# A routed-expert stage: 4 KB weight runs, low parts on VectorE, earlier gathers, and two accumulators taken by turns

## The chip, the cores and the metric

The kernel runs on one core of a Trainium2 chip. A core has TensorE (PE in the profile; PEld is its loading of the stationary operand), VectorE (DVE), ScalarE (ACT), GpSimd (POOL) and SyncE (SP), each with an instruction queue of its own that it works through in order, and 16 DMA engines that all queues share. The metric is the device time of one execution in microseconds (us); times given are medians of several runs.

## The reference

One encoder block of width 1024 over 1024 tokens: a mixer (a long convolution and a state-space branch, gated), a layer norm, a mixture of 64 experts with a shared expert, and a second layer norm. The change touches the mixture and the last norm. Every token picks 8 of 64 experts; an expert has three matrices, gate and up of 1024x256 and down of 256x1024.

```
def step(acc, blk):
    tok, wt, e = blk
    xb = h_pad[tok]
    hb = jax.nn.silu(xb @ w_gate[e]) * (xb @ w_up[e])
    yb = (hb @ w_down[e]) * wt[:, None]
    return acc.at[tok].add(yb.astype(acc.dtype)), None

ffn = routed + shared
h = layer_norm(DN_ALPHA * h + ffn, ln2_g[i], ln2_b[i])
```

All of it is float32, 3 MB of weights for each expert, 201 MB in all.

## The kernel before

The kernel runs the mixer, then a merge stage (`merge`, with the shared expert and the router inside it), then the expert stage (`moe`), then the last norm. Float32 products are made from rounded operands: each operand is split into a high part (a rounded copy, made by ScalarE) and a low part (the operand less its high part), and a product of two operands is three matmuls, high by high, high by low and low by high (`mm3`, L76; called from L78 to L80 in the profile).

The expert stage runs 96 blocks of token rows. The experts are sorted by load and get fixed capacities of 192, 160, 128 and 112 rows. An expert of 192 or 160 rows makes two blocks, of 128 and of 64 or 32 rows; the others make one. `order` takes a heavy and a light expert by turns, so three blocks (128 rows, 64 or 32 rows, 128 or 112 rows) and two experts form a group that repeats 32 times. A small block packs high and low tokens into one stationary operand and needs two matmuls in place of three (`both_mm`, L1857; L1860 to L1863).

The weights of expert i come as three pieces of 1 MB, numbered p = 3i, 3i+1, 3i+2: half of gate and up, the other half, and down. `w_load(p)` (L1584) reads the expert's number into a register, issues the DMAs and fills one of six `eraw` buffers. For gate and up it writes 256 gate columns and 256 up columns of a row next to each other, so each contiguous run is 1 KB. Gate and up are issued by SP, down by POOL. `w_hi(p)` (L1602) makes the high part on ScalarE, and `w_lo(p)` (L1613) the low part, on VectorE for gate and up and on POOL for down.

`gather(b)` (L1620) fetches a block's rows from `h` in HBM by an indirect DMA from POOL into one of three `xg` buffers. `xpose(b)` (L1629) turns them on TensorE (L1640) and splits them. `swi_gu` and `both_gu` do gate and up (8 steps k), `swi_act` and `both_act` the activation, `hidden(b)` (L1645) turns and splits the result `hb`, and `down(b)` (L1650 to L1663) makes the output rows `yo` (two buffers) and adds them to `acc` in HBM by an indirect DMA from POOL that reads, adds and writes. A scatter waits until the one before it has landed, since both touch `acc`. `slot_tables` (L2056) makes the row numbers of eight experts at a time, a step in each block, on VectorE and TensorE.

Every engine's order is the order of the code in this stage (`manual_schedule`). In iteration b of the loop at L1718 it is: gather(b+3); high parts of pieces 2b+2 and 2b+3; gate and up of block b, and after k = 3 the low part of 2b+2, the load of 2b+8 and hidden(b-1); the activation of b; xpose(b+2); the low part of 2b+3 and the load of 2b+9; one table step; down(b-1) with its scatter.

The last norm (L1750 on) loads the 8 row tiles of `acc` (4.2 MB) as `fx` and, tile by tile, takes statistics, centres, scales and stores. Ahead of the stage, `early` (L1674) loads the first three pieces, makes the first tables and gathers block 0 while the merge stage still runs.

Of the kernel before, what the change touches and what calls it, by code (L numbers as in the profile page):

```python
# [41 lines left out]
class Kern:  # L42
# [1167 lines left out]
    def merge(self):  # L1210
# [5 lines left out]
        self.acc_d = self.scratch("acc", (L + P, D))  # L1216
        p1 = tc.alloc_tile_pool(name="mg", bufs=1, reuse_waits="tile")
# [99 lines left out]
        with ExitStack() as cx:  # L1317
# [138 lines left out]
            def sh_gu(t):  # L1456
                gu = [sh[k // 2][k % 2] for k in range(8)]
                for k, ps in enumerate(self.swi_gu(lhs(t), gu, P)):
                    if k < 7:
                        yield  # L1460
                yield self.swi_act(pool, ps, P, ld()[:, 0:256])
# [100 lines left out]
    def moe(self):  # L1562
# [3 lines left out]
        with ExitStack() as cx:  # L1566
# [17 lines left out]
            def w_load(p):  # L1584
                if p >= 192:
                    return
                i, q = divmod(p, 3)
                eng = nc.gpsimd if q == 2 else nc.sync
                if q != 1:
                    weng[0] = eng.value_load(self.eid[0:1, order[i]:order[i] + 1], min_val=0, max_val=63)  # L1590
                g, u, d = [a[n][0][bass.ds(weng[0], 1)].rearrange("o (p j) c -> (o p) j c", p=P)
                           for n in ("exp_w_gate", "exp_w_up", "exp_w_down")]
                parts = ((g[:, 0:4], u[:, 0:4]), (g[:, 4:8], u[:, 4:8]), (d,))[q]
                wraw[p] = rps[i % 2].tile([P, 2048], F32, name="eraw", bufs=3)
                v = wraw[p].rearrange("p (k c) -> p k c", k=parts[0].shape[1])
                c0 = 0
                for src in parts:
                    n = src.shape[2]
                    eng.dma_start(v[:, :, c0:c0 + n], src)
                    c0 += n  # L1600

            def w_hi(p, c=slice(0, 2048)):  # L1602
                if p >= 192:
                    return
                if p not in whl:
                    i, q = divmod(p, 3)
                    hi, lo = whl[p] = [wps[i % 2].tile([P, 2048], F32R, name=f"e{c}", bufs=3) for c in ("hi", "lo")]
                    k = 2 if q == 2 else 4
                    wsplit.setdefault(i, []).extend(zip(*[[v.rearrange("p (k c) -> p k c", k=k)[:, j] for j in range(k)]
                                                          for v in (hi, lo)]))  # L1610
                nc.scalar.copy(whl[p][0][:, c], wraw[p][:, c])  # L1611

            def w_lo(p, c=slice(0, 2048)):  # L1613
                if p >= 192:
                    return
                eng = nc.gpsimd if p % 3 == 2 else nc.vector
                hi, lo = whl[p]
                eng.tensor_tensor(lo[:, c], wraw[p][:, c], hi[:, c].bitcast(F32), ALU.subtract)  # L1618
# [31 lines left out]
            def down(b):  # L1650
# [3 lines left out]
                y = pool.tile([P, D], F32, name="yo", bufs=2)  # L1654
                wd = [[(h[:, q * 512:(q + 1) * 512], l[:, q * 512:(q + 1) * 512]) for q in range(2)] for h, l in wsplit[i][8:10]]
                if n in (32, 64):
                    self.both_down(hbs.pop(b), wd, y, n)
                else:
# [3 lines left out]
                    out=self.acc_d, out_offset=bass.IndirectOffsetOnAxis(ap=tabs[r][s][1], axis=0),  # L1662
# [11 lines left out]
            def early(oh):  # L1674
                er = tc.alloc_tile_pool(name="er0", bufs=1, side="right")
                rps.append(er)
                for p in range(3):
                    w_load(p)
                for _ in self.slot_tables(er, groups[0], tabs, 2, oh):
                    yield 2  # L1680
                gather(0)
                for _ in self.slot_tables(er, groups[1], tabs, 2, oh):
                    yield 3
# [20 lines left out]
            for p in range(3, 6):  # L1704
                w_load(p)
            xpose(0)
            for p in range(2):
                for c in [slice(c * 512, c * 512 + 512) for c in range(4)]:
                    w_hi(p, c)
                    w_lo(p, c)  # L1710
                w_load(p + 6)
            xpose(1)
            tj = iter(())

            def lo_load(p):
                w_lo(p)
                w_load(p + 6)
            for b, (i, r, s, o, n) in enumerate(blocks):  # L1718
# [5 lines left out]
                gather(b + 3)  # L1724
# [3 lines left out]
                for k, ps in enumerate((self.both_gu if n in (32, 64) else self.swi_gu)(x, gu, n)):  # L1728
                    if k == 3:
                        lo_load(2 * b + 2)  # L1730
                        hidden(b - 1)
# [4 lines left out]
                xpose(b + 2)  # L1736
                lo_load(2 * b + 3)
# [17 lines left out]
            for i in range(8):  # L1755
                nc.sync.dma_start(xs[i], self.acc_d[i * P:(i + 1) * P, :])
# [5 lines left out]
            def stats(i, h):  # L1762
                if h == 0:
                    st[i] = pool.tile([P, 2, 6], F32, name="f_st", bufs=2)
                nc.vector.bn_stats(st[i][:, h, :], xs[i][:, h * 512:(h + 1) * 512])  # L1765
# [57 lines left out]
    def swi_gu(self, lhs, gu, n):  # L1823
        ps = self.bank()
        for k in range(8):
            self.mm3(ps[:n, :], lhs[k][0], lhs[k][1], gu[k][0], gu[k][1], k == 0, k == 7)
            yield ps
# [37 lines left out]
    def both_gu(self, x, gu, n):  # L1865
        ps = self.bank()
        for k in range(8):
            self.both_mm(ps, x[:, k], n, gu[k][0], gu[k][1], k == 0, k == 7)
# [502 lines left out]
```

## Time and profile before

| | us |
|---|---|
| median of 3 runs | 3530.07 (3528.78 to 3532.55) |
| the profiled execution | 3534.84 |
| its span, first to last instruction | 3533.2 |
| PE, DVE, ACT, POOL busy over the span | 3188.0, 2590.6, 1406.7, 1676.7 |
| experts, from the first expert matmul to the last scatter's issue | 2395 to 3479 |
| last norm | 3479 to 3533 |

The profile comes from one execution, with a trace of every instruction and DMA packet. Busy shares say how much of a stretch an engine worked; what sets the time of a stretch is read from the idle time ahead of an instruction and from what released it. The clock column is the share of TensorE's full speed that was granted: 1.0 is 2.4 GHz, 0.5 is 1.2 GHz.

### The profile page before, as it was taken

The numbers are of one execution on the slowest core, as the hardware profiler recorded it, in microseconds if no ns is written. First come the engines' busy times: TensorE is split into PE (matmuls) and PEld (weight loads), VectorE is DVE, ScalarE is ACT, GpSimd is POOL, SyncE is SP. The second block draws the span as 40 slices with busy tenths as digits, with TensorE's granted clock in tenths as the row PEclk, the third lists the DMA queues.
The fourth block names the chain that finished last, engine by engine and source line by source line (L and its number), as shares of the span: only waits on it lengthen the run. The fifth ranks groups of instructions, "written<-read, shape, count | busy, mean of one in ns | idle before, by whom it ended". The sixth has DMA issues, their size and how long they took to land. (4 is left out here: it accounts for less than half of the span.)

```text
span 3533.2 us, 42386 instructions
## 1 busy us (share of the span) xinstructions
PE 3188.0 (90%) x14923; PEld 2506.6 (71%) x14923; DVE 2590.6 (73%) x3551; ACT 1406.7 (40%) x2206; POOL 1676.7 (47%) x1480
## 2 busy tenths in 40 slices
PE   8989998989998998899999999997889888888893
PEld 6767776777777777567888888875666666666662
DVE  6787887888787878557994344657778787677786
ACT  3334333343334232322223212415656555565663
POOL 2545454555454546441110320215667667777774
PEclk9999899999999999899999999988999999899996
DMA  4323232322322322744325445327999899888894
GB/s 131 78 72 87 67 96 75 85 73 79 91 78 75 89 72 91 215 147 151 106 90 173 126 155 158 107 85 242 271 271 270 259 259 262 250 249 249 250 283 128
DMA packets 439908, 538.22 MB, mean 152 GB/s; under 512 B 24361, under 2 KB 373325, under 8 KB 430989
## 3 DMA queue, kind: packets, MB, share of 16 engines
q1 hardware_dynamic: 404717, 379.23, 36.6%
q0 software_dynamic: 33824, 152.06, 15.0%
q10 hardware_dynamic: 1152, 4.19, 0.3%
q8 instruction: 119, 1.95, 0.2%
q14 instruction: 96, 0.79, 0.1%
HBM read 430.29 MB, written 105.12 MB: 152 GB/s over the span
## 5 line engine op out<-in xcount | busy, mean ns | idle before, releaser
L170 PE MATMUL bankA<-xth,whi 128*128 128x512 f32 (+1 forms) x1424 | 470.1, 412 | 0.5 <-ACT whi L73 0.3
L170 PE MATMUL bankA<-xtl,whi 128*128 128x512 f32 (+1 forms) x1424 | 452.6, 400 | 0.0
L170 PE MATMUL bankA<-xth,wlo 128*128 128x512 f32 (+1 forms) x1424 | 449.4, 397 | 1.5 <-POOL wlo L74 1.5
L1618 DVE TENSOR_TENSOR elo<-eraw,ehi 128x2048 fp32r<-128x2048 f32 (+1 forms) x134 | 393.7, 2945 | 18.9 <-ACT ehi L1611 13.1
L1661 POOL DMA_INDIRECT scr_acc<-yo,sidx x96 | 231.1, 2407 | 275.9 <-DMA scr_acc<-yo,sidx 147.1
L1611 ACT CAST ehi<-eraw 128x2048 fp32r<-128x2048 f32 (+1 forms) x198 | 356.3, 1852 | 3.3 <-DMA eraw<-in_exp_w_gate_dram 3.3
L74 POOL TENSOR_TENSOR wlo<-wraw,whi 128x1024 fp32r<-128x1024 f32 (+1 forms) x89 | 225.4, 2532 | 278.1 <-ACT whi L73 278.1
L170 PEld LDWEIGHTS bankA<-xtl,whi 128*128 128x128 f32 (+1 forms) x1424 | 274.5, 193 | 64.1 <-DVE xtl L74 0.4
L170 PEld LDWEIGHTS bankA<-xth,wlo 128*128 128x128 f32 (+1 forms) x1424 | 272.2, 191 | 64.5 <-POOL wlo L74 2.0
L170 PEld LDWEIGHTS bankA<-xth,whi 128*128 128x128 f32 (+1 forms) x1424 | 268.2, 195 | 58.3 <-issue 5.4
L1618 POOL TENSOR_TENSOR elo<-eraw,ehi 128x2048 fp32r<-128x2048 f32 x64 | 298.1, 4658 | 15.8 <-ACT ehi L1611 14.7
L399 POOL TENSOR_SCALAR Wm<-cbm,dt 128x128 f32<-128x128 f32 x256 | 129.9, 507 | 348.2 <-DVE cbm L373 348.2
L1625 POOL DMA_INDIRECT xg<-scr_h,gidx x96 | 182.3, 1899 | 63.4 <-issue 24.3
L79 PE MATMUL bankA<-elo,xgh 128*128 128x512 f32 (+1 forms) x512 | 203.6, 398 | 8.6 <-DVE elo L1618 8.6
L78 PE MATMUL bankA<-ehi,xgh 128*128 128x512 f32 (+1 forms) x512 | 210.1, 410 | 0.0
L80 PE MATMUL bankA<-ehi,xgl 128*128 128x512 f32 (+1 forms) x512 | 203.3, 397 | 0.0
L1640 PE MATMUL bankB<-ident,xg 128*128 128x128 f32 (+3 forms) x768 | 113.4, 295 | 94.0 <-DMA xg<-scr_h,gidx 92.5
L1640 PEld LDWEIGHTS bankB<-ident,xg 128*128 128x128 f32 (+3 forms) x768 | 101.5, 198 | 122.9 <-issue 107.5
L74 DVE TENSOR_TENSOR xgl<-bankB,xgh 128x512 fp32r<-128x512 f32 (+1 forms) x128 | 81.3, 664 | 107.7 <-ACT xgh L73 106.0
L80 PE MATMUL bankA<-ehi,hb 128*128 128x512 f32 (+1 forms) x256 | 121.3, 474 | 27.0 <-DVE hb L74 26.9
L1877 DVE SCALAR_TENSOR_TENSOR lows<-lows,wt 64x256 f32<-64x256 f32 (+1 forms) x32 | 132.5, 4140 | 15.5 <-ACT lows L1876 15.5
L393 DVE SCALAR_TENSOR_TENSOR Em<-bcs,Acs,Em 128x128 f32<-128x128 f32 x256 | 140.9, 609 | 2.3
(551 smaller groups left out, 7672.7 us busy)
## 6 DMA issues: line engine op xcount, KB each, us to landing
eraw<-in_exp_w_gate_dram SPq DMA_DIRECT2D x128, 512.0 KB, 5.9
eraw<-in_exp_w_down_dram POOLq DMA_DIRECT2D x64, 1024.0 KB, 6.0
eraw<-in_exp_w_up_dram SPq DMA_DIRECT2D x128, 512.0 KB
wraw<-in_w_in_dram SPq DMA_DIRECT2D x88, 512.0 KB, 4.1
bcs<-scr_at SPq DMA_DIRECT2D x128, 256.0 KB, 5.6
scr_K<-kout SPq DMA_DIRECT2D x32, 512.0 KB, 2.8
Kt<-scr_K SPq DMA_DIRECT2D x32, 512.0 KB, 3.5
scr_gate<-accf SPq DMA_DIRECT2D x16, 512.0 KB, 4.2
```

The costliest lines, as they stand in the source:

```text
L74: (lo_eng or nc.vector).tensor_tensor(lo, src, hi.bitcast(F32), ALU.subtract)
L78: mm(out, sh, mh, start=first, stop=False)
L79: mm(out, sh, ml, start=False, stop=False)
L80: mm(out, sl, mh, start=False, stop=last)
L170: mm(ps[h], wt[:, k, :n], x[:, h * 512:(h + 1) * 512], start=(k == 0 and f == 1), stop=(k == KT - 1 and l == 1))
L393: STT(E[:, h], bcs[:, 1, h], self.A[:, c, 32 + j:33 + j], E[:, h], ALU.subtract, ALU.min)
L1611: nc.scalar.copy(whl[p][0][:, c], wraw[p][:, c])
L1618: eng.tensor_tensor(lo[:, c], wraw[p][:, c], hi[:, c].bitcast(F32), ALU.subtract)
L1625: nc.gpsimd.indirect_dma_start(out=t[:n, :], out_offset=None, in_=self.h_d, in_offset=bass.IndirectOffsetOnAxis(ap=tabs[r][s][0], axis=0))
L1640: nc.tensor.transpose(ps[:, j * P:j * P + n], free(t[:n, k:k + 1], [[8, P]]), self.ident[:n, :n])
L1661: nc.gpsimd.indirect_dma_start(out=self.acc_d, out_offset=bass.IndirectOffsetOnAxis(ap=tabs[r][s][1], axis=0), in_=y[:n, :], in_offset=Non ...
L1877: nc.vector.scalar_tensor_tensor(t[:, 0:256], t[:, 0:256], w, t[:, 256:512], ALU.mult, ALU.mult)
```

## The change

1. Gate and up land in the buffer as one run each: a partition's 4 rows of 256 columns stay together, 4 KB to a run, gate ahead of up. The matmuls read the moving operand as two runs of 256 columns (`"p (s k c) -> p k s c"`); the shared expert's views get the same shape.
2. All three pieces are issued by SP, and all low parts are made by VectorE.
3. `eraw` has five buffers instead of six (the load of p+5 follows the low part of p); `yo` has four instead of two.
4. gather(b+5) stands behind xpose(b+2), in place of gather(b+3) at the iteration's start; two more gathers precede the loop.
5. hidden(b-1) stands ahead of the low part of 2b+2. In the two blocks of every eighth expert a second table step runs after k = 5.
6. Blocks scatter by turns into `acc` (odd b) and a new `ace` (even b), which is filled with zeros ahead of the stage: one memset and 8 stores of 512 KB. The zeros lie in the `xg` buffer that gather(0) uses.
7. The last norm loads 8 tiles of `ace` and then 8 of `acc`, and adds them on VectorE in 16 instructions of 128x512.

```
-                eng = nc.gpsimd if q == 2 else nc.sync
-                if q != 1:
+                eng = nc.sync
+                if q == 0:
...
-                wraw[p] = rps[i % 2].tile([P, 2048], F32, name="eraw", bufs=3)
-                v = wraw[p].rearrange("p (k c) -> p k c", k=parts[0].shape[1])
-                c0 = 0
-                for src in parts:
-                    n = src.shape[2]
-                    eng.dma_start(v[:, :, c0:c0 + n], src)
-                    c0 += n
+                wraw[p] = rps[p % 5 // 3].tile([P, 2048], F32, name="eraw", bufs=3 - p % 5 // 3)
+                v = wraw[p].rearrange("p (s k c) -> p s k c", s=len(parts), k=parts[0].shape[1])
+                for n, src in enumerate(parts):
+                    eng.dma_start(v[:, n], src)
...
-                eng = nc.gpsimd if p % 3 == 2 else nc.vector
                 hi, lo = whl[p]
-                eng.tensor_tensor(lo[:, c], wraw[p][:, c], hi[:, c].bitcast(F32), ALU.subtract)
+                nc.vector.tensor_tensor(lo[:, c], wraw[p][:, c], hi[:, c].bitcast(F32), ALU.subtract)
...
-                y = pool.tile([P, D], F32, name="yo", bufs=2)
+                y = pool.tile([P, D], F32, name="yo", bufs=4)
...
-                    out=self.acc_d, out_offset=bass.IndirectOffsetOnAxis(ap=tabs[r][s][1], axis=0),
+                    out=self.acc_d if b % 2 else self.ace_d,
+                    out_offset=bass.IndirectOffsetOnAxis(ap=tabs[r][s][1], axis=0),
...
+                z = er.tile([P, D], F32, name="xg")
+                nc.gpsimd.memset(z, 0.0)
+                for t in range(8):
+                    nc.sync.dma_start(self.ace_d[t * P:(t + 1) * P, :], z)
...
             def lo_load(p):
                 w_lo(p)
-                w_load(p + 6)
+                w_load(p + 5)
...
-                gather(b + 3)
...
                     if k == 3:
+                        hidden(b - 1)
                         lo_load(2 * b + 2)
-                        hidden(b - 1)
+                    if k == 5 and i % 8 == 0:
+                        next(tj, None)
...
                 xpose(b + 2)
+                gather(b + 5)
                 lo_load(2 * b + 3)
...
-            for i in range(8):
-                nc.sync.dma_start(xs[i], self.acc_d[i * P:(i + 1) * P, :])
+            xe = [pool.tile([P, D], F32, name="fe", bufs=8) for _ in range(8)]
+            for v, d in ((xe, self.ace_d), (xs, self.acc_d)):
+                for i in range(8):
+                    nc.sync.dma_start(v[i], d[i * P:(i + 1) * P, :])
...
-                nc.vector.bn_stats(st[i][:, h, :], xs[i][:, h * 512:(h + 1) * 512])
+                c = slice(h * 512, (h + 1) * 512)
+                TT(xs[i][:, c], xs[i][:, c], xe[i][:, c], ALU.add)
+                nc.vector.bn_stats(st[i][:, h, :], xs[i][:, c])
```

## Rows read from the trace of the kernel before

**Rows 1.** Windows: us, busy us of each engine (x instructions), PEclk, DMA share, GB/s.

```profile
2430.00:3430.00 1000.00, 879.35 (x4430) 661.91 (x4429) 772.68 (x762) 597.29 (x746) 701.50 (x298) 0.93 0.89 259
2600.00:2700.00 100.00, 88.56 (x428) 67.85 (x426) 78.72 (x76) 59.91 (x73) 72.00 (x31) 0.93 0.94 274
```

**Rows 2.** Window of the merge stage, ahead of the experts.

```profile
1500.00:2200.00 700.00, 696.83 (x3066) 556.55 (x3065) 428.21 (x575) 169.40 (x329) 131.35 (x115) 1.00 0.43 139
```

**Rows 3.** Groups by line, 2430 to 3430: busy us, mean ns, idle before.

```profile
L1618 DVE TENSOR_TENSOR elo<-eraw,ehi 128x2048 fp32r<-128x2048 f32 x120 | 363.5, 3032 | 13.2 <-ACT ehi L1611 13.1
L1611 ACT CAST ehi<-eraw 128x2048 fp32r<-128x2048 f32 x180 | 333.5, 1904 | 0.0
L1618 POOL TENSOR_TENSOR elo<-eraw,ehi 128x2048 fp32r<-128x2048 f32 x59 | 272.5, 4619 | 1.1
L1661 POOL DMA_INDIRECT scr_acc<-yo,sidx x90 | 218.4, 2427 | 255.6 <-DMA scr_acc<-yo,sidx 147.1 <-DVE sg L1834 25.9 <-ACT yo L1660 22.5
L1625 POOL DMA_INDIRECT xg<-scr_h,gidx x90 | 176.1, 1956 | 27.6 <-issue 23.4 <-PE bankB L1640 3.7 <-PE bankA L80 0.3
L1877 DVE SCALAR_TENSOR_TENSOR lows<-lows,wt 64x256 f32<-64x256 f32 (+1 forms) x29 | 124.4, 4291 | 14.1 <-ACT lows L1876 14.1
```

**Rows 4.** Waits, 2430 to 3430: us in total, times, longest.

```profile
POOL scr_acc L1661 <- DMA scr_acc<-yo,sidx: 147.1, 32, 8.0
DVE xgl L74 <- ACT xgh L73: 104.0, 33, 6.2
PE bankB L1640 <- DMA xg<-scr_h,gidx: 91.2, 35, 5.5
PE bankA L80 <- DVE hb L74: 18.6, 17, 1.9
```

**Rows 5.** Timeline: start us, us, engine, line, operation, [idle before <-releaser].

```profile
2427.22 0.48 DVE L1877 SCALAR_TENSOR_TENSOR lows<-lows,wt 64x256 f32<-64x256 f32 x1 [0.48 <-ACT lows L1876]
2902.72 4.59 POOL L1661 DMA_INDIRECT scr_acc<-yo,sidx  x1 [0.84 <-DMA scr_acc<-yo,sidx]
2903.54 2.27 DVE L1618 TENSOR_TENSOR elo<-eraw,ehi 128x2048 fp32r<-128x2048 f32 x1
2916.50 1.46 POOL L1661 DMA_INDIRECT scr_acc<-yo,sidx  x1 [6.41 <-DMA scr_acc<-yo,sidx]
```

**Rows 6.** Timeline of PE in two stretches with hardly a wait.

```profile
2430.64 0.43 PE L78 MATMUL bankA<-ehi,xgh 128*128 128x512 f32 x1
2436.92 1.09 PE L1640 MATMUL bankB<-ident,xg 64*128 64x64 f32 x8
2440.08 0.40 PE L78 MATMUL bankA<-ehi,xgh 128*128 128x512 f32 x1
...
3418.83 1.12 PE L1640 MATMUL bankB<-ident,xg 112*128 112x112 f32 x8 [0.22 <-DMA xg<-scr_h,gidx]
3422.57 0.39 PE L1861 MATMUL bankA<-ehi,xgh 128*64 128x512 f32 x1
3426.70 1.13 PE L1640 MATMUL bankB<-ident,xg 128*128 128x128 f32 x8
```

**Rows 7.** DMA queues, 2450 to 3350: packets, MB, share of 16 engines.

```profile
q0 software_dynamic: 26059, 121.11, 46.0%
q1 hardware_dynamic: 112143, 111.37, 43.2%
```

**Rows 8.** DMA queues, 3490 to 3497: the final loads, 4 KB rows.

```profile
q1 hardware_dynamic: 781, 2.88, 101.5%
```

**Rows 9.** Timeline and window of the tail.

```profile
3485.47 3.76 SPq L1756 DMA_DIRECT2D fx<-scr_acc  x8
3490.00:3494.00 4.00, 0.00 (x0) 0.00 (x0) 3.81 (x13) 0.44 (x2) 0.00 (x0) 0.50 1.00 402
```

**Rows 10.** Window and timeline of PE ahead of the stage.

```profile
2372.00:2376.00 4.00, 4.00 (x42) 3.31 (x41) 2.97 (x3) 0.00 (x0) 0.00 (x0) 1.00 0.01 2
2369.26 0.38 PE L1640 MATMUL bankB<-ident,xg 128*128 128x128 f32 x2
```

More of the change, by code (lines that the diff above doesn't have):

```diff
@@ L1216, in merge @@
         self.acc_d = self.scratch("acc", (L + P, D))
+        self.ace_d = self.scratch("ace", (L + P, D))
         p1 = tc.alloc_tile_pool(name="mg", bufs=1, reuse_waits="tile")
@@ L1456, in sh_gu @@
             def sh_gu(t):
-                gu = [sh[k // 2][k % 2] for k in range(8)]
+                gu = [[v.rearrange("p (s c) -> p s c", s=2) for v in sh[k // 2][k % 2]] for k in range(8)]
                 for k, ps in enumerate(self.swi_gu(lhs(t), gu, P)):
@@ L1607, in w_hi @@
                     hi, lo = whl[p] = [wps[i % 2].tile([P, 2048], F32R, name=f"e{c}", bufs=3) for c in ("hi", "lo")]
-                    k = 2 if q == 2 else 4
-                    wsplit.setdefault(i, []).extend(zip(*[[v.rearrange("p (k c) -> p k c", k=k)[:, j] for j in range(k)]
+                    k, n = (2, 1) if q == 2 else (4, 2)
+                    wsplit.setdefault(i, []).extend(zip(*[[v.rearrange("p (s k c) -> p k s c", s=n, k=k)[:, j] for j in range(k)]
                                                           for v in (hi, lo)]))
@@ L1653, in down @@
                 i, r, s, o, n = blocks[b]
-                y = pool.tile([P, D], F32, name="yo", bufs=2)
-                wd = [[(h[:, q * 512:(q + 1) * 512], l[:, q * 512:(q + 1) * 512]) for q in range(2)] for h, l in wsplit[i][8:10]]
+                y = pool.tile([P, D], F32, name="yo", bufs=4)
+                wd = [[(h[:, 0, q * 512:(q + 1) * 512], l[:, 0, q * 512:(q + 1) * 512]) for q in range(2)] for h, l in wsplit[i][8:10]]
                 if n in (32, 64):
@@ L1703, in moe @@
             gather(2)
-            for p in range(3, 6):
+            for p in range(3, 5):
                 w_load(p)
             xpose(0)
+            gather(3)
             for p in range(2):
@@ L1710, in moe @@
                     w_lo(p, c)
-                w_load(p + 6)
+                w_load(p + 5)
             xpose(1)
+            gather(4)
             tj = iter(())
@@ L1716, in lo_load @@
                 w_lo(p)
-                w_load(p + 6)
+                w_load(p + 5)
             for b, (i, r, s, o, n) in enumerate(blocks):
@@ L1824, in swi_gu @@
         ps = self.bank()
+        p3 = ps[:n, :].rearrange("p (s c) -> p s c", s=2)
         for k in range(8):
-            self.mm3(ps[:n, :], lhs[k][0], lhs[k][1], gu[k][0], gu[k][1], k == 0, k == 7)
+            self.mm3(p3, lhs[k][0], lhs[k][1], gu[k][0], gu[k][1], k == 0, k == 7)
             yield ps
@@ L1866, in both_gu @@
         ps = self.bank()
+        p3 = ps.rearrange("p (s c) -> p s c", s=2)
         for k in range(8):
-            self.both_mm(ps, x[:, k], n, gu[k][0], gu[k][1], k == 0, k == 7)
+            self.both_mm(p3, x[:, k], n, gu[k][0], gu[k][1], k == 0, k == 7)
             yield ps
```

## The prediction

> **What bounds the kernel now.** I read the windows first, to see which stage the change touches and whether any engine is full there. From 2430 to 3430 us the stage is in its steady state: 90 of its 96 blocks, by the 90 gathers [rows 3], so 30 groups of three blocks in 1000 us, 33.3 us each. PE is busy 879 us, DVE 773, POOL 702, ACT 597, the DMA engines 0.89, the granted clock 0.93 [rows 1]. Nothing is full, so the time lies in waits.
>
> The second view is a dense piece of PE's timeline, which gives the floor. A big block's gate and up take 6.28 us from their first matmul to the transposes behind them, and from there to the next block's first matmul (transposes, a table step, a small down) 3.16 us, 9.44 us together. A small block's gate and up take 4.13 us, and transposes with a big down 3.74 us [rows 6]. A group has one iteration of each kind: 9.44, 6.28 + 3.74 = 10.02, and 4.13 + 3.74 = 7.87, so 27.3 us without a wait.
>
> The third view is the list of waits: it must account for 33.3 - 27.3 = 6.0 us. PE waits for gathered rows 91.2 us in 30 groups, 3.0 each, and for `hb` 18.6 us, 0.6 each [rows 4]. The clock is the rest: 0.93 in place of 1.00 is 7% of 33.3, 2.3 us. The sum is 5.9. In the merge stage, where PE is busy 697 of 700 us, the clock is 1.00 [rows 2]; it falls in the expert stage, where PE waits.
>
> Why do rows come late? POOL's queue. It waits 147.1 us for an earlier scatter to land, at most 8.0 at once [rows 4]; 6.41 us before the one at 2916.50 [rows 5]. A gather stands behind it in POOL's queue, and so do POOL's low parts, 4.62 us each [rows 3]. A second effect is on VectorE: a low part takes 2.27 us where POOL makes none [rows 5] but 3.03 on average, and the product in `both_act` 0.48 us [rows 5] against 4.29 on average [rows 3]. Both read two SBUF operands and are held while POOL makes its own.
>
> **The change, part by part.**
>
> *Two accumulators, early gathers, four `yo` buffers.* A scatter now waits for the one two blocks back, about 20 us earlier, so the 147 us go. gather(b+5) leaves three iterations ahead of its use instead of nearly two. It gains a wait, on xpose(b+2), which frees its buffer; the scatter of b-1 queues behind that, and its data come later anyway. With some 28 us of lead I take the 3.0 us wait for rows as gone. Late next are `hb`, the clock and the DMA engines.
>
> *Low parts of down on VectorE.* It adds 59 x 2.27 = 134 us in the window. It removes the holding: 120 x (3.03 - 2.27) = 91 us, and 29 x (4.29 - 0.48) = 110 us [rows 3, 5]. VectorE's work falls from 772.7 / 30 = 25.8 to 23.5 us a group, and POOL's from 23.4 to 14.3. PE's cover for a low part is one iteration, as before. Placing hidden(b-1) ahead of a low part takes 2.27 us from the path to `hb`, but ScalarE's two high parts (1.90 us each [rows 3]) still stand ahead of it, so I keep the whole 0.6 us. The spaced table steps add no work; if one pushes the next `hb` back, its 0.6 us doubles, and the DMA term below still ends later.
>
> *4 KB runs, down on SP, five `eraw` buffers.* From 2450 to 3350 us (27 groups) queue q1, gate and up, holds the DMA engines for 43.2% and q0 for 46.0% [rows 7]: 14.4 and 15.3 us a group, 29.7 together. Per MB q1 costs 0.432 x 900 x 16 / 111.37 = 55.9 engine-us. The final loads, in 4 KB rows with nothing beside them, cost 1.015 x 7 x 16 / 2.88 = 39.5 [rows 8]. The price among scatters is in no row: between 39.5 (q1 falls to 10.2) and 55.9 (no gain). A gain beyond the first is excluded, since that stretch had no rival traffic; a loss I exclude too, as each run only has fewer ends. I take the middle, as the second figure contains queueing, which stays: q1 12.3 and 27.6 a group, ends 25.5 and 29.7. The Trainium skill, "DMA: Bandwidth & Descriptors", section Specifications, gives 512 B as the smallest transfer at line rate, by which 1 KB and 4 KB runs cost the same and the sum would be rival A's; the rows here mix run length with company and don't decide it. The highest share of the DMA engines over 100 us is 0.94 [rows 1]; at that the group needs 29.4 us, ends 27.1 and 31.6. Down moves to SP's queue at the same bytes. SP waits for VectorE's low part before each load, and what queues behind it are later loads alone. The shortest lead is now 1.3 iterations, about 13 us; ScalarE's high parts wait 0.0 us for weights today [rows 3], so I price the sixth buffer at nothing. The matmuls' view has one break in 512 columns. The nearest row, transposes with a stride at every element, 8 in 1.09 us [rows 6], runs on without gaps, so nothing there either.
>
> *Sum for a group.* PE: 27.3 + 0.6 for `hb` + a third of the clock's 2.3, since most of its falls follow the waits for rows, 0.8: 28.7. DMA: 29.4. The later counts: 29.4, so 3.9 us saved, times 32 groups, 125 us.
>
> *Ahead of the stage.* Eight zero stores (4.2 MB) go out behind the first weights, where the DMA engines are idle, share 0.01 [rows 10]: nothing. But gather(0) now waits for them, and PE turns its rows at 2369 us, in front of merge matmuls [rows 10]. If that order stays, PE could stand until about 2388, 19 us; if the compiler's order moves too, nothing. I take nothing; 19 is the upper end. A gain is excluded.
>
> *The tail.* The norm's first tile needs the ninth load instead of the first. Loads start at 3485.47 and run at up to 402 GB/s [rows 9], so 4.19 MB cost 10.4 us. If the `ace` loads pass ahead of the last scatter, nothing. Sixteen additions: a quarter of a low part, 0.57 us [rows 5], is the lower end; with some overhead 0.65, so 10.4 us. VectorE leads there, busy 3.81 of 4 us [rows 9], and nothing hides them. Tail: +21, ends +9 and +28 (two holds by POOL's additions, 3.6 us each, on top).
>
> **Sum.** 3534.8 - 125 + 21 = 3431 for a profiled run. The profiled run lies 4.8 us over the median of 3530.07, so 3426. Low: a group at 28.0 saves 170, tail +9, so 3369. High: a group at 31.6 saves 54, tail +21, so 3497; a late start as well is rarer than the range needs.
>
> **The rivals.**
>
> *A. The DMA engines keep their price.* Per byte nothing is gained, 29.7 us a group stays, and at a share of 0.94 a group takes 31.6: 3530 - 54 + 21 = 3497. For it: rows of 1 KB may have cost 55.9 because scatters hold the engines, not because they are short. Against it: 39.5 alone. The rule above gives this result.
>
> *B. VectorE's waits stay.* It is idle 227 us in the window, 7.6 a group, mostly for ScalarE (104.0 us for `xgl` alone [rows 4]). If this is a fixed chain and not the echo of PE's late rows, a group is 23.5 + 7.6 = 31.1: 3530 - 70 + 21 = 3481. Against it: the longest such wait, 6.2 us, is as long as PE's wait for rows.
>
> *C, slower: POOL starves.* An indirect DMA's descriptors take 1.46 us alone and 4.59 beside VectorE's low part [rows 5]. VectorE now makes all low parts. If each of a group's six indirect DMAs met two of them, 1.46 + 2 x 2.27 = 6.0 us, POOL would need 36 us a group: +86 + 21, 3637. It decides from 5.4 us on average (32.7 us a group, where the tail is not paid back); now the averages are 2.43 and 1.96 [rows 3]. The Trainium skill, "SBUF — State Buffer", section SBUF: two separate sides, calls the port pair that VectorE and GpSimd share an exclusive lock, held for the whole instruction, and warns that VectorE's work can starve descriptors. [...]
>
> *D, slower: the chains don't part.* If both accumulators' scatters still follow one another, in the queue they share, groups stay at 33.3 and the tail is paid: 3551. Nothing in the trace speaks for it but the common queue.
>
> **How the numbers follow.** Forecast 0.58, A 0.17, B 0.12, C 0.05, D 0.05; 0.03 for a time within 0.2% (7 us), about what a measurement of this kernel can tell from no change. Faster: 0.58 + 0.17 + 0.12 = 0.87. Slower: 0.10. The range takes in the forecast's ends, B and A: 3369 to 3500.
>
> **What would show it.** POOL's wait for its own scatter gone, PE's wait for rows near zero, and the clock above 0.97 between 2430 and the stage's end: the first step. Low parts on VectorE all near 2.27 us and its product near 0.48: the second. q1's engine time per MB between 40 and 56: the third; at 56, rival A. The first VectorE instruction of the tail some 10 us later after the last scatter, and 16 additions of about 0.65 us. Indirect DMAs on POOL above 5 us would be rival C. I am wrong if a new wait of PE, for `hb` or for weights, exceeds 2 us a group.

## The result and the profile after

The changed kernel takes 3417.36 us (median of four runs, 3410.85 to 3420.2); the kernel before took 3529.43 beside it (3517.78 to 3532.55). The ratio is 0.9686, 95% interval 0.966 to 0.9712: 3.1% faster. Predicted were 3426 us with a range of 3369 to 3500. The profiled run took 3410.85 us at a span of 3409.1.

The windows of the changed kernel show its steady stage and the slice that answers to [rows 1]; the columns are as there.

```profile
2430.00:3330.00 900.00, 861.40 (x4540) 656.26 (x4537) 717.89 (x846) 608.86 (x773) 377.58 (x183) 0.98 0.95 295
2600.00:2700.00 100.00, 93.98 (x510) 73.73 (x509) 79.33 (x78) 68.13 (x85) 40.67 (x20) 0.98 0.96 299
```

PE's share goes from 0.88 to 0.96, the clock from 0.93 to 0.98, the DMA share from 0.89 to 0.95. POOL falls from 0.70 to 0.42. Groups by line, same stretch (busy us, mean ns, idle before and its releasers), answer to [rows 3]:

```profile
L1615 DVE TENSOR_TENSOR elo<-eraw,ehi 128x2048 fp32r<-128x2048 f32 x185 | 422.0, 2281 | 0.0
L1622 POOL DMA_INDIRECT xg<-scr_h,gidx x89 | 185.1, 2080 | 160.0 <-PE bankB L1637 149.3 <-PE bankD L2091 5.3 <-DMA eraw<-in_exp_w_up_dram 4.5
L1658 POOL DMA_INDIRECT scr_acc<-yo,sidx x47 | 99.7, 2122 | 179.7 <-ACT yo L1657 106.6 <-DVE yo L1911 65.8 <-DMA scr_ace<-yo,sidx 7.2
L1889 DVE SCALAR_TENSOR_TENSOR lows<-lows,wt 32x256 f32<-32x256 f32 (+1 forms) x31 | 14.7, 475 | 15.0 <-ACT lows L1888 15.0
```

In the first 820 us (the last blocks have no gather beside them) there are 85 gathers and 84 scatters, so 28.9 to 29.3 us a group of three blocks, where it was 33.3; I take 29.1. PE's own transposes give the group more exactly: from the seventh block's to the 91st's, 28 groups, they take 943.5 us before (2454.3 to 3397.8) and 816.5 after (2446.1 to 3262.6), 33.7 and 29.2 a group. Low parts take 2281 ns and the product 475, where they took 3032 and 4291. The waits, same stretch (us in total, times, longest), answer to [rows 4]:

```profile
DVE hb L74 <- ACT hb L73: 154.3, 86, 5.2
PE bankD L2091 <- DVE oh L2083: 36.6, 12, 3.9
POOL scr_ace L1658 <- DMA scr_acc<-yo,sidx: 8.1, 1, 8.1
POOL scr_acc L1658 <- DMA scr_ace<-yo,sidx: 7.2, 1, 7.2
PE bankA L78 <- ACT hb L73: 1.6, 2, 0.8
```

PE waits for rows no more, and hardly for `hb`. Its wait for `oh`, the comparison on VectorE from which PE makes a table, has grown. In the kernel before, from 2430 to 3430 us, it was small:

```profile
PE bankD L2079 <- DVE oh L2071: 5.9, 7, 1.6
```

POOL's 147 us for its own scatters are 15. The DMA queues from 2450 to 3250 us (packets, MB, share of 16 engines) answer to [rows 7]:

```profile
q1 hardware_dynamic: 39390, 171.77, 62.3%
q0 software_dynamic: 18884, 66.61, 33.4%
```

The end of the stage and the tail, from the timeline, answer to [rows 9]:

```profile
3332.36 1.48 POOL L1658 DMA_INDIRECT scr_acc<-yo,sidx  x1 [2.32 <-ACT yo L1657]
3339.22 4.54 SPq L1764 DMA_DIRECT2D fe<-scr_ace  x8
3343.80 9.19 SPq L1764 DMA_DIRECT2D fx<-scr_acc  x8
3353.96 0.69 DVE L1774 TENSOR_TENSOR fx<-fx,fe 128x512 f32<-128x512 f32 x1 [25.23 <-DMA fx<-scr_acc]
```

The same scatter of the kernel before:

```profile
3478.70 1.48 POOL L1661 DMA_INDIRECT scr_acc<-yo,sidx  x1 [2.97 <-ACT yo L1660]
```

The last scatter leaves 146.3 us earlier. From there to the end of the span it is 76.7 us, where it was 54.5: 22.2 given back. 146.3 - 22.2 = 124.1, the difference of the spans.

### The profile page after: what moved, and what is told of

It reads as the page before. It is cut to its first block, busy times and chain, and to the rows that moved or that the text cites. A ratio compares the mean times of both kernels' runs of the same rounds, so it can differ in the third digit from the quotient of the medians.

```text
span 3409.1 us, 42239 instructions
## 1 busy us (share of the span) xinstructions
PE 3131.7 (92%) x14922; PEld 2471.0 (72%) x14923; DVE 2522.5 (74%) x3631; ACT 1399.5 (41%) x2206; POOL 1318.4 (39%) x1353
## 4 chain that ended last, share of the span: by engine, by line
PE 52%; DVE 29%; ACT 6%; issue 6%; POOL 4%; DMA 3%; SPq 0%; ACTq 0%; DVEq 0%; POOLq 0%
PE bankA L78 7%; PE bankA L1293 7%; PE bankA L80 7%; PE bankA L79 7%; PE bankA L170 5%; DVE yt L430 3%; DVE Em L393 3%; PE bankI L1091 3%; PE bankA L1035 3%; DVE accxs L178 2%; PE bankA L1872 2%; PE bankB L1637 2%; ACT ehi L1609 1%; PE bankA L1874 1%; DVE accf L178 1%
## 5 line engine op out<-in xcount | busy, mean ns | idle before, releaser
L1615 DVE TENSOR_TENSOR elo<-eraw,ehi 128x2048 fp32r<-128x2048 f32 (+1 forms) x198 | 438.3, 2217 | 2.5 <-DMA scr_acc<-sr 2.5
L1622 POOL DMA_INDIRECT xg<-scr_h,gidx x96 | 193.3, 2014 | 212.2 <-PE bankB L1637 166.7
L399 POOL TENSOR_SCALAR Wm<-cbm,dt 128x128 f32<-128x128 f32 x256 | 129.8, 507 | 348.2 <-DVE cbm L373 348.2
L1658 POOL DMA_INDIRECT scr_acc<-yo,sidx x48 | 101.2, 2108 | 182.0 <-ACT yo L1657 109.0
L1658 POOL DMA_INDIRECT scr_ace<-yo,sidx x48 | 94.7, 1973 | 191.0 <-ACT yo L1657 112.7
L74 DVE TENSOR_TENSOR hb<-bankC,hb 128x256 fp32r<-128x256 f32 (+3 forms) x96 | 34.8, 363 | 156.6 <-ACT hb L73 156.3
L430 DVE TENSOR_TENSOR yt<-yt,off 128x256 f32<-128x256 f32 x112 | 134.0, 1196 | 3.9
L394 ACT ACTIVATE Em<-Em 128x512 f32<-128x512 f32 x64 | 40.4, 631 | 225.1 <-DVE Em L393 225.1
L400 POOL TENSOR_SCALAR Wm<-cbm,dt 128x128 f32<-128x128 f32 x256 | 126.9, 496 | 0.0
L1035 PE MATMUL bankA<-sdf,Fm 128*128 128x256 f32 x512 | 124.2, 386 | 1.6 <-DVE U L1052 1.6
```

The costliest lines, as they stand in the source:

```text
L74: (lo_eng or nc.vector).tensor_tensor(lo, src, hi.bitcast(F32), ALU.subtract)
L430: TT(y, y, off[:, d], ALU.add)
L1035: mm(out, Fm[:, fy, mt, fs], sd[:, ty, mt], start=mt == 0, stop=mt == 1 and not edge)
L1615: nc.vector.tensor_tensor(lo[:, c], wraw[p][:, c], hi[:, c].bitcast(F32), ALU.subtract)
L1658: nc.gpsimd.indirect_dma_start(out=self.acc_d if b % 2 else self.ace_d, out_offset=bass.IndirectOffsetOnAxis(ap=tabs[r][s][1], axis=0), in ...
```

## The experiments

Each kernel differs from the changed kernel, or from the one before, by the diff shown. Ratios are to the kernel before on the same chip.

| kernel | median us | ratio | 95% interval |
|---|---|---|---|
| changed kernel | 3417.4 | 0.9686 | 0.966 to 0.9712 |
| changed, low parts of down on POOL again | 3532.1 | 1.0003 | 0.9991 to 1.0015 |
| before, low parts of down on VectorE | 3434.9 | 0.9719 | 0.9696 to 0.9742 |
| changed, low parts on POOL, product from PSUM | 3461.7 | 0.9804 | 0.9788 to 0.982 |
| before, product from PSUM | 3489.4 | 0.9881 | 0.9864 to 0.9897 |
| changed, late gathers | 3508.8 | 0.9936 | 0.9918 to 0.9954 |
| changed, late gathers, old order at k = 3 | 3432.4 | 0.9734 | 0.9695 to 0.9773 |
| changed, one accumulator | 3411.4 | 0.9665 | 0.9632 to 0.9699 |
| changed, 1 KB runs | 3417.3 | 0.9688 | 0.9653 to 0.9723 |
| changed, table step at k = 2 | 3372.3 | 0.9549 | 0.9516 to 0.9582 |
| the same, one accumulator | 3400.1 | 0.9611 | 0.9595 to 0.9627 |
| the same, 1 KB runs | 3370.3 | 0.9529 | 0.9513 to 0.9545 |
| the same, tail loads in turns | 3360.1 | 0.9506 | 0.9488 to 0.9523 |

**Where the low part is made.** First undone alone, then done alone.

```diff
+                eng = nc.gpsimd if p % 3 == 2 else nc.vector
                 hi, lo = whl[p]
-                nc.vector.tensor_tensor(lo[:, c], wraw[p][:, c], hi[:, c].bitcast(F32), ALU.subtract)
+                eng.tensor_tensor(lo[:, c], wraw[p][:, c], hi[:, c].bitcast(F32), ALU.subtract)
```

> The changed kernel with one thing undone: the low part of each block's down weights is made on POOL again, as before. Theory: VectorE and POOL hold each other whenever both read two SBUF operands. The mean low part on VectorE goes from 2.28 back to about 3.0 us, its product in `both_act` from near 0.5 to over 4 us, POOL's indirect DMAs queue behind 4.6 us of low part each, and PE gets a wait for `hb` or rows of 1 to 3 us a group: 30 to 95 us more, 3447 to 3512 us. Rival: the holding is off the path, since PE sets the pace and VectorE has 26% of its time idle: within 10 us of the changed kernel's 3417.

Measured: 3532 us, nothing left of the gain. Groups by line of this kernel, 2430 to 3250 us:

```profile
L1616 DVE TENSOR_TENSOR elo<-eraw,ehi 128x2048 fp32r<-128x2048 f32 x99 | 244.6, 2471 | 0.0
L1616 POOL TENSOR_TENSOR elo<-eraw,ehi 128x2048 fp32r<-128x2048 f32 x49 | 240.3, 4904 | 0.5
L1890 DVE SCALAR_TENSOR_TENSOR lows<-lows,wt 64x256 f32<-64x256 f32 (+1 forms) x24 | 106.2, 4423 | 11.6 <-ACT lows L1889 11.6
L2084 DVE TENSOR_TENSOR oh<-iota,posm 128x1024 bf16<-128x1024 int16 (+1 forms) x50 | 93.7, 1875 | 0.0
```

PE's waits of the same stretch:

```profile
PE bankC L1898 <- DVE lows L1890: 47.0, 18, 2.7
PE bankD L2092 <- DVE oh L2084: 43.3, 12, 3.9
```

PE waits for no rows here, and POOL does not wait for scatters; still the time is that of before. The product on VectorE takes 4423 ns beside POOL's low part, and PE waits for it instead, 2.6 us at a time, and for `oh`: 90.3 us in 820. In the same stretch of the kernel before PE waited for rows and `hb`:

```profile
PE bankB L1640 <- DMA xg<-scr_h,gidx: 72.8, 30, 5.5
PE bankA L80 <- DVE hb L74: 17.1, 16, 1.9
```

With 5.9 for `oh` that is 95.8. The two kernels stand at the same time for different reasons. Part of it is the tail: from the first gate and up to the last down PE takes 1061.6 us here and 1081.4 in the kernel before, and from the last scatter to the end it is 75.6 us here and 54.5 there. So the other parts of the change gain 20 us in the stage, and the tail gives 21 back. The expected 30 to 95 us were too few by 20, and low parts on VectorE slowed less than expected (2471, not 3000).

In the kernel before:

```diff
-                eng = nc.gpsimd if p % 3 == 2 else nc.vector
+                eng = nc.vector
```

> The kernel before with one thing changed: the low part of each block's down weights is made on VectorE, as the other low parts are. One accumulator, 1 KB runs, late gathers, two result buffers and the issue of down's loads on POOL stay. Theory, from the run that put this part back on POOL (3532 us, nothing left of the gain): this edit alone carries the change. PE's waits for rows and `hb` go, and the time is within 20 us of the changed kernel's 3417, so 3397 to 3437. Rival: it is necessary but not enough. With gathers issued about two iterations ahead, behind POOL's wait for the earlier scatter and for VectorE before down's load, PE still waits for rows by 1 us a group or more, and the time is 3450 us or more.

Measured: 3435 us, 0.9719. This edit alone brings 2.8 of the 3.1%. In the stage, without the tail, it is less of the whole: from the first gate and up to the last down PE takes 973.9 us, where it was 1081.4 and is 932.8 in the changed kernel. But the rival's sign is there too. PE's and POOL's waits, 2430 to 3250 us:

```profile
PE bankB L1640 <- DMA xg<-scr_h,gidx: 49.8, 26, 4.9
POOL eraw L1599 <- ACT ehi L1611: 132.6, 26, 5.5
POOL scr_acc L1661 <- DMA scr_acc<-yo,sidx: 74.7, 13, 8.6
```

Rows are still awaited for 49.8 us, 1.8 a group.

**What is held.** This is tried in the kernel with POOL's low parts first. The edit makes the product in `both_act` read one operand from PSUM; the computation is the same.

```diff
-        nc.vector.tensor_tensor(t, t, ps[0:n], ALU.add)
-        nc.scalar.activation(t[:, 0:256], t[:, 0:256], AF.Silu)
-        nc.vector.scalar_tensor_tensor(t[:, 0:256], t[:, 0:256], w, t[:, 256:512], ALU.mult, ALU.mult)
+        nc.vector.tensor_tensor(ps[0:n], t, ps[0:n], ALU.add)
+        nc.scalar.activation(t[:, 0:256], ps[0:n, 0:256], AF.Silu)
+        nc.vector.scalar_tensor_tensor(t[:, 0:256], t[:, 0:256], w, ps[0:n, 256:512], ALU.mult, ALU.mult)
```

> The changed kernel with the low parts of down back on POOL (the run at 3532 us), and one more edit: in `both_act` the sum of the two halves is written to PSUM, so that the product reads one operand from SBUF and one from PSUM, in place of two from SBUF. Theory: what PE waited for with the low parts on POOL was this product, held for 4.4 us each time; the wait for `lows` (47 us in 820) and the dips of the clock behind it go, and with the held table comparisons left the time falls by 60 to 110 us, to 3420 to 3470. Rival: the hold only moves on, to the next VectorE instruction with two SBUF operands or to POOL's queue, and PE waits as long for it: 3500 us or more.

Measured: 3462 us, 70 less than the run without this edit. Groups by line, 2430 to 3250 us:

```profile
L1616 DVE TENSOR_TENSOR elo<-eraw,ehi 128x2048 fp32r<-128x2048 f32 x108 | 293.4, 2717 | 0.0
L2084 DVE TENSOR_TENSOR oh<-iota,posm 128x1536 bf16<-128x1536 int16 (+1 forms) x52 | 135.8, 2611 | 0.0
L1890 DVE SCALAR_TENSOR_TENSOR lows<-lows,wt,bankA 64x256 f32<-64x256 f32 (+1 forms) x26 | 12.2, 471 | 11.5 <-ACT lows L1889 11.5
```

PE's largest wait of the same stretch:

```profile
PE bankD L2092 <- DVE oh L2084: 54.1, 12, 5.4
```

The product takes 471 ns with POOL's low parts still there, and PE's wait for it is gone: the hold was on the second SBUF operand, and it was on the path. The rival is half right as well. Over the free times of 2281, 475 and 1485 ns, low parts, products and `oh` were held 18.8 + 94.8 + 19.5 = 133 us; now it is 47 + 0 + 59 = 106. The hold moved on, to places where less hangs on it. What these rows show agrees with the Trainium skill, "SBUF — State Buffer", section Who interferes with whom, by which a VectorE instruction with at most one SBUF input, outside its two-port modes, stays clear of GpSimd, and one with two contends with a GpSimd instruction that reads SBUF.

The same edit in the kernel before:

> The kernel before with one thing changed, the same edit of `both_act`: the product reads one operand from PSUM. POOL keeps its low parts, one accumulator and late gathers. Theory of the held product: it sits between a block's gate and up and its `hb`, so without the 4.3 us hold the chain through VectorE and ScalarE gets shorter, `yo` and the scatters come earlier, and PE's wait for rows shrinks: 3430 to 3490 us. Rival, POOL's queue (the prediction's first step): rows come late because scatter, low part and gather stand one behind another on POOL; that stays, and the time is within 20 us of 3530.

Measured: 3489 us, 0.9881, at the upper end of the theory's range. PE's waits, 2430 to 3250 us:

```profile
PE bankB L1640 <- DMA xg<-scr_h,gidx: 37.1, 22, 3.6
PE bankA L80 <- DVE hb L74: 34.5, 23, 5.5
```

Those for rows fall from 72.8, and those for `hb` rise from 17.1. So half of the wait for rows hung on the held product, and some of what it freed turned into the wait for `hb`.

**Early gathers and the order at k = 3.**

```diff
-            gather(3)
...
-            gather(4)
...
+                gather(b + 3)
                 w_hi(2 * b + 2)
...
-                    if k == 5 and i % 8 == 0:
-                        next(tj, None)
...
-                gather(b + 5)
```

> The changed kernel with its early gathers undone: gather(b+3) at the start of an iteration as before, and with it no extra table step, which only the early gathers need (they use the next table before the old point at which it is finished). Two accumulators, 4 KB runs, low parts on VectorE and four result buffers stay. Theory: with low parts off POOL and no wait for an earlier scatter, a gather leaves within some 4 us of its iteration's start and lands 9 us after that, before the end of the next iteration, where its rows are turned. PE then waits for neither rows nor tables: 3375 us within 10, as with the table step moved. Rival: the early gathers are needed. PE waits for rows by 1 us a group or more, as in the run of before with its low parts on VectorE (1.8 us a group): 3400 us or more.

Measured: 3509 us. The theory missed by 134, the rival holds: early gathers are needed, in this kernel. PE's, POOL's and VectorE's waits, 2430 to 3250 us:

```profile
PE bankB L1637 <- DMA xg<-scr_h,gidx: 76.5, 27, 4.1
POOL scr_acc L1658 <- ACT yo L1657: 187.3, 25, 11.4
DVE hb L74 <- ACT hb L73: 137.8, 60, 5.6
```

POOL waits for `yo`, not for scatters, and the gather stands behind the scatter. From the timeline I read a loop: PE turns rows, makes down, `yo` follows, then scatter, gather, and two iterations on PE turns those rows. It would be as long as its steps, whatever else is free; no run tests the loop by itself. But the kernel before with low parts on VectorE has late gathers too, and takes 3435. What made the loop longer here? The next kernel has the late gathers too, and the old order at k = 3:

```diff
                     if k == 3:
-                        hidden(b - 1)
                         lo_load(2 * b + 2)
+                        hidden(b - 1)
```

> The changed kernel with late gathers, as in the run at 3509 us, and one more part undone: at k = 3 the first low part is made before `hidden`, as in the kernel before. Open is why late gathers cost 92 us here, where the kernel before with its low parts on VectorE and the same late gathers takes 3435. Theory: the new order. VectorE's split into `hb` now stands ahead of the low part and waits 2.3 us each time for ScalarE's high parts (138 us in 820); the low part and all behind it, `lows` and `yo` among them, come that much later, and with late gathers `yo`, scatter, gather and the turned rows form a loop of two iterations. With the old order: 3420 to 3450 us, and VectorE's wait for `hb` is gone. Rival: another part (4 KB runs, down's loads on SP with five buffers, two accumulators) lengthens the loop: within 15 us of 3509, with PE's waits for rows still at 3 us a group.

Measured: 3432 us, 76 less than with the new order. PE's largest wait and VectorE's, 2430 to 3250 us:

```profile
PE bankB L1637 <- DMA xg<-scr_h,gidx: 40.0, 26, 3.6
DVE elo L1615 <- ACT ehi L1609: 48.7, 39, 3.3
```

The wait for `hb` is gone from VectorE. The new order costs 76 us where gathers are late. This kernel has two accumulators, 4 KB runs, four `yo` and down's loads on SP, and is as fast as the kernel before with its low parts on VectorE alone (0.9734 and 0.9719, intervals overlapping): with late gathers these four bring nothing to the time. That is a gain and a loss: the last scatter leaves 20.2 us earlier (3350.91 against 3371.14), and from there to the end it is 75.8 us in place of 54.7, 21.1 more, for the second accumulator's loads and additions. Early gathers with the old order were not tried.

**One accumulator.**

```diff
-                    out=self.acc_d if b % 2 else self.ace_d,
+                    out=self.acc_d,
...
-                TT(xs[i][:, c], xs[i][:, c], xe[i][:, c], ALU.add)
```

The buffer `ace`, its zero stores and its loads in the tail go with it.

> The changed kernel with one accumulator again: no `ace`, no zero stores, no `ace` loads in the tail and none of its 16 additions; everything else of the change stays. Theory: in the changed kernel an indirect scatter lands 8.4 us after its issue (median), so three of them one after another need about 26 us, less than the 29.2 us that a group now takes, and POOL has time to wait. The stage stays as it is, and the tail gives back its 22 us: about 3395 us, 0.993 of the changed kernel. Rival, the step of the prediction: one accumulator brings POOL's waits for its own earlier scatter back, the gathers queue behind them, and PE waits for rows again. Then the stage loses a good part of its 147 us of waits, and the time is above 3440 us, with PE waiting over 30 us in all for gathered rows.

Measured: 3411 us, not to be told from 3417. POOL's largest wait, 2430 to 3250 us:

```profile
POOL scr_acc L1658 <- DMA scr_acc<-yo,sidx: 137.4, 23, 10.4
```

The last two scatters, from the timeline:

```profile
3349.51 1.33 POOL L1658 DMA_INDIRECT scr_acc<-yo,sidx  x1 [5.61 <-DMA scr_acc<-yo,sidx]
3353.71 1.48 POOL L1658 DMA_INDIRECT scr_acc<-yo,sidx  x1 [2.87 <-DMA scr_acc<-yo,sidx]
```

The wait that the prediction set out to remove is back, 137 us of it, and still PE waits for no rows: its one wait there is for `oh`, 36.6 us. The tail is 54.7 us again, 22.0 less. But the last scatter leaves 21.4 us later (3353.71 against 3332.36). Of these, 5.8 are a later start (first gate and up at 2404.29, in place of 2398.53), which I did not follow; 6.8 are a longer stage (939.6 us to the last down, in place of 932.8); and 8.8 are the last scatters, one behind another: the last leaves 9.9 us behind PE's last down, in place of 1.0. Theory and rival both missed: the gain of the tail is spent ahead of it.

The same edit with the table step at k = 2 (that diff is below):

> The changed kernel with one accumulator and the table step at k = 2 together. Theory: the two are independent, so the 45 us of the table step and the 6 us of the single accumulator add: about 3366 us. Rival: with PE at 27.9 us a group, three chained scatters of 8 to 9 us each leave POOL too little time, rows come late again and PE waits for them: 3385 us or more, above the 3372 of the table step alone.

The rival is right: 3400 us, 0.9611 against 0.9549, some 22 us more than with two accumulators. PE waits for rows again, and POOL for its scatters, 2430 to 3250 us:

```profile
PE bankB L1637 <- DMA xg<-scr_h,gidx: 25.6, 14, 4.9
POOL scr_acc L1658 <- DMA scr_acc<-yo,sidx: 176.3, 32, 9.7
```

So one chain of scatters is enough for groups of 29 us and too slow for 27.6.

**4 KB runs.**

```diff
-                v = wraw[p].rearrange("p (s k c) -> p s k c", s=len(parts), k=parts[0].shape[1])
+                v = wraw[p].rearrange("p (k s c) -> p s k c", s=len(parts), k=parts[0].shape[1])
...
```

The matmuls' view of the pieces changes with it.

> The changed kernel with one thing undone: the weights arrive in SBUF in runs of 1 KB again, at the same bytes, from the same queue and with the same work on them. Theory: a byte in short runs costs more engine time. Before, the DMA engines needed 55.2 engine-us per MB over both queues, after it 51.4; at the old price the 28.0 us of DMA time that a group needs become 30.1, and at a share of 0.96 the group takes 31.3 in place of 29.2: about +67 us, 3485; if all of the difference lies on the weights (55.9 against 46.4), up to +120. Rival: run length costs nothing, as PE sets the pace or as the engines move 1 KB at the same rate: within 10 us of 3417, with the weights' queue at 46 engine-us per MB again.

Measured: 3417.3 us, no difference; the rival is right. The queues from 2450 to 3250 us:

```profile
q1 hardware_dynamic: 122091, 170.27, 64.9%
q0 software_dynamic: 18758, 66.17, 33.2%
```

q1 costs 0.649 x 800 x 16 / 170.27 = 48.8 engine-us per MB with 1 KB runs and 46.4 with 4 KB: 5%. A third of q1's bytes is down, which the edit leaves as it is; from the packets of gate and up alone it is 51.1 against 47.4, 8%. The difference is paid in a share of 0.98 in place of 0.96, and in no time.

The same edit with the table step at k = 2:

> The changed kernel with the table step at k = 2 and the weights in 1 KB runs. With the table step alone a group takes 27.9 us, PE is busy 99% and the DMA engines' share is 1.00. Theory: PE sets the pace; a share of 1.00 says that some packet is always under way, not that no more would fit. Then the 5% more engine time that 1 KB runs cost change nothing: 3372 us within 8. Rival: at a share of 1.00 the DMA engines are the bound. 5% of the weights' 17.9 us of engine time in a group are 0.9 us, times 32: 3400 us or more, with PE waiting for weights or rows.

Measured: 3370 us, beside 3372. The windows, 4 KB and 1 KB runs, both with the table step at k = 2. First 4 KB:

```profile
2430.00:3250.00 820.00, 810.83 (x4369) 620.43 (x4369) 692.09 (x817) 583.67 (x740) 413.09 (x178) 1.00 1.00 314
```

then 1 KB:

```profile
2430.00:3250.00 820.00, 810.77 (x4381) 620.08 (x4380) 691.75 (x818) 586.19 (x742) 414.87 (x178) 1.00 1.03 315
```

The share is 1.00 and 1.03 at the same rate. PE is busy 99% and waits for no transfer: PE sets the pace.

**The table step.**

```diff
+                    if k == 2 and i % 8 == 0:
+                        next(tj, None)
                     if k == 3:
                         hidden(b - 1)
                         lo_load(2 * b + 2)
-                    if k == 5 and i % 8 == 0:
-                        next(tj, None)
```

> The changed kernel with the extra table step of an iteration made at k = 2, ahead of the hidden products, in place of k = 5, behind them and behind VectorE's low part. Theory: in the changed kernel PE sets the pace, and every 118 us it loses 6.1 us in two waits for the table's `oh`, which VectorE makes behind a 2.28 us low part, and some more in the clock's dips that follow. With `oh` made earlier both go: 7 to 8 times 6 to 8 us, 45 to 65 us less, 3355 to 3375 us. Rival: the DMA engines set the pace (28.0 us of 29.2 a group); then the waits only move to weights or rows, and the gain is at most half: 3390 us or more.

Measured: 3372 us, 45 less, at the lower end of what was expected of a PE-bound stage. The timeline of the changed kernel shows the wait that goes:

```profile
2649.77 0.42 DVE L74 TENSOR_TENSOR hb<-bankC,hb 128x256 fp32r<-128x256 f32 x1 [3.50 <-ACT hb L73]
2650.11 2.28 DVE L1615 TENSOR_TENSOR elo<-eraw,ehi 128x2048 fp32r<-128x2048 f32 x1
2652.31 1.75 DVE L2083 TENSOR_TENSOR oh<-iota,posm 128x1536 bf16<-128x1536 int16 x1
2654.12 0.87 PE L2091 MATMUL bankD<-aux,oh 128*128 128x6 bf16 x16 [3.85 <-DVE oh L2083]
```

`oh` stands behind the low part, which stands behind `hb`, and PE idles 3.85 us. With the step at k = 2 PE's wait for `oh` is 9.2 us in 820 in place of 36.6, and the clock is 1.00:

```profile
PE bankD L2091 <- DVE oh L2083: 9.2, 6, 1.6
```

**The tail.** With the table step at k = 2:

```diff
-            for v, d in ((xe, self.ace_d), (xs, self.acc_d)):
-                for i in range(8):
-                    nc.sync.dma_start(v[i], d[i * P:(i + 1) * P, :])
+            for i in range(8):
+                for v, d in ((xe, self.ace_d), (xs, self.acc_d)):
+                    nc.sync.dma_start(v[i], d[i * P:(i + 1) * P, :])
```

> The changed kernel with the table step at k = 2 and the 16 loads of the tail in the order ace 0, acc 0, ace 1, acc 1 and so on, in place of all of `ace` first. Theory: the first addition then needs two loads in place of nine, the next tiles arrive faster than VectorE takes them, and the tail is shorter by the time of seven loads, about 9 us: 3363 us. Rival: VectorE's chain of work is not what ends the tail, or the last scatter into `ace` holds the first load back as long: 3372 within 4.

Measured: 3360 us, 10 less than the 1 KB kernel on the same chip and 12 less than the 4 KB one. The first addition:

```profile
3297.16 0.34 SPq L1764 DMA_DIRECT2D fe<-scr_ace  x1
3297.56 0.42 SPq L1764 DMA_DIRECT2D fx<-scr_acc  x1
3302.20 0.69 DVE L1774 TENSOR_TENSOR fx<-fx,fe 128x512 f32<-128x512 f32 x1 [15.36 <-DMA fx<-scr_acc]
```

It comes 5.0 us after the first load, 14.7 in the changed kernel. This is the fastest kernel of the study, 0.9506 of before.

## Why the prediction was right, and where it was not

The time was right, 9 us off, and so was the sign. The term that carried it was not.

*The floor.* Right. 27.3 us a group was read from stretches of before. With the table step at k = 2 and the clock at 1.00, 89 gathers in 820 us make 27.6 a group, of which 9.2 / 29.7 = 0.3 is the wait for `oh`.

*Two accumulators.* The step "a scatter now waits for the one two blocks back, so the 147 us go" failed as a cause. The 147 us went; with one accumulator 137 us of such waits in 820 are there, and PE hardly feels them: its stage is 6.8 us longer. A queue's wait was taken for PE's wait because it was long and the gather stood behind it. What was late lay, as I read the timeline, in a loop through VectorE, ScalarE and POOL. Three things hung in it: the product held by POOL's low part, the low part in POOL's own queue, and a gather issued behind the scatter. The runs show the first (1.2% in the kernel before) and the third (late gathers cost 92 us with the new order, 15 with the old); the second is what is left over, with the holds of the other VectorE instructions, and no run parts it from them. Taking POOL's low parts away gives 2.8% alone, and all the other parts without it give nothing (1.0003), as their 20 us in the stage go to the tail. PE's stage in the profiled executions, first gate and up to last down, shows the order of size: 1081.4 us before, 973.9 with low parts on VectorE, 953.9 with two accumulators, 4 KB runs, four `yo` and down's loads on SP as well, 932.8 with early gathers, the new order and the spaced table steps. So low parts bring 107 us, and the other parts 41, of which the tail takes 22.

*Low parts on VectorE.* The durations were right (2281 and 475 ns for 2.27 and 0.48). The size was not: the step booked 201 us of holding as VectorE's load, which didn't limit, and nothing in the sum hung on it. It was worth about 100 to 115 us.

*`hb` and the new order.* The 0.6 us a group kept for `hb` is hardly there: 2.0 us in 900, less than 0.1 a group. The order was priced as a gain of nothing; with late gathers it costs 76 us.

*Table steps.* "Add no work" is true and was not the question. PE waits 36.6 us for `oh` in 900, 1.2 a group (30.9 groups of 29.1), and the clock falls behind it; the whole is 45 us. The condition at the end, a new wait of PE above 2 us a group, was not reached.

*The clock.* 0.98: 0.6 us of 29.1, for 0.8 predicted.

*The DMA term.* "29.4 counts" failed. The need was right, (0.623 + 0.334) x 800 us over 800 / 29.1 = 27.5 groups is 27.8 for 27.6 predicted (its reason was half right, see below), but the ceiling of 0.94 was only the highest share seen before; 1.00 and 1.03 followed without a wait. PE's own sum, 27.3 + 1.2 + 0.6 = 29.1, is what the group takes. That the DMA term came to 29.4 is chance.

*The price of 1 KB runs.* The price forecast for gate and up in 4 KB runs, 12.3 / 14.4 x 55.9 = 47.7 engine-us per MB, came out: 47.4. But run length is only 3.7 of the 8.5 that the price fell from 55.9: in the changed kernel 1 KB runs cost 51.1, and where the other 4.8 come from I did not find. So the choice of the middle met the number by luck, with half of the reason. Rival A was right that rows of 1 KB cost 55.9 in part for their company; its need of 29.7 us a group did not stay, and its time of 3497 failed with the same ceiling. The Trainium skill, "DMA: Bandwidth & Descriptors", section Specifications, with 512 B as the smallest transfer at line rate, agrees nearly: the rows show 5% over the queue and 8% on gate and up, not nothing.

*Start and tail.* The last scatter leaves 146.3 us earlier for 125 forecast. The groups explain it: by PE's transposes they took 33.7 and 29.2 us, and 127.0 us in 28 groups are 145 in 32. The 33.3, a count of 90 gathers in 1000 us, was 0.4 too low, so the account of the waits, 5.9 us, left 0.5 of 6.4 open. The start cost hardly anything, though PE turns its first rows 21.7 us later (2390.96 for 2369.26): its first gate and up comes 2.9 us later (2398.53 for 2395.61). The tail gave back 22.2 for 21. VectorE's first instruction comes 21.6 us after the last scatter in place of 10.3, 11.3 more for 10.4 forecast; twelve of the additions take 0.67 to 0.69 us, and four, beside POOL's additions, 2.1 to 2.7.

*The other rivals.* B: VectorE still waits, 154 us for `hb` in 900, and PE doesn't wait for it, so its group of 31.1 fell. C: indirect DMAs took 1.97 to 2.12 us on average, not 5.4. VectorE's low parts seem to lengthen them: in the kernel before, from 2430 to 3250 us, 28 scatters with no low part beside them took 1.45 us on average, 27 with one 2.57, 18 with two 3.97, though a long one also meets more of them. The 4.59 us is no case of the warning that the prediction sets beside it: the Trainium skill, "SBUF — State Buffer", section SBUF: two separate sides, tells of starved descriptors beside VectorE's two-port modes, and by its section Who interferes with whom a `tensor_tensor`, as a low part is, has no such mode. D: the chains parted, two waits of 7 and 8 us remained.

## What to carry to other kernels

A long wait in a queue is not yet the wait that ends the group: follow it until it reaches the engine that sets the pace, or take away what it waits for and see; here one accumulator brought 137 us of it back, and PE's stage grew by 7. When two limits stand at the same time, undoing either half of a change can cost all of it, so parts are to be tried both alone and left out. A part that gains in one stage and pays in another can show as nothing in the time, so each stage is to be read by itself. An operation that adds no work can still cost where it stands, if the engine that sets the pace waits behind it.

## What was not expected of the hardware

A VectorE product of 64x256 with both operands in SBUF took 4423 ns beside POOL's low part and 471 with one operand in PSUM, with POOL as busy as before. The DMA engines' share went to 1.03 with PE, VectorE and ScalarE waiting for no transfer: at 0.94 it was no ceiling. Gate and up in runs of 1 KB cost 51.1 engine-us per MB where 4 KB cost 47.4, and the time was the same.
